# A two-block model on one core: the convolution's running sum, the norm's reciprocal and the one-hots' row of numbers move to PSUM, and the gates' copy writes runs of four

## The chip, the cores and the metric

The kernel runs on one core of a Trainium2 chip. TensorE (PE) multiplies matrices and writes to the PSUM memory; VectorE (DVE), ScalarE (ACT) and GpSimd (POOL) do elementwise work on SBUF and PSUM (POOL, here, on SBUF only); SyncE (SP) and ACT issue most DMAs. The metric is the device time of one execution in microseconds.

## The reference, cut to what matters

The model has 512 tokens of width 1024 and two blocks. The first block's mixer has a causal convolution of 31 taps over 384 channels, followed by a layer norm; then come a mixture of 32 experts, and the second block with two recurrent mixers (on more tokens of context) and a product-key expert layer. The two parts that the change touches:

```python
def hybrid_mixer(x, w_in, conv_a_w, conv_a_b, ln_a_g, ln_a_b, ...):
    z = x @ w_in
    a_val, a_gate, b_gate, c_gate, b_val, pool_in = jnp.split(z, IN_SPLITS, axis=-1)
    u = a_val * jax.nn.sigmoid(a_gate)
    u = causal_depthwise_conv(u, conv_a_w) + conv_a_b          # 31 taps, 384 channels
    y_a = jax.nn.silu(layer_norm(u, ln_a_g, ln_a_b))
    ...
    return jnp.concatenate([y_a, y_b, y_c], axis=-1) @ w_out

def _peer(h, w_query, sub_keys, expert_u, expert_v):           # 8 heads, 128 x 128 experts, 16 chosen per head
    q = (t @ w_query).reshape(n_tok, P_HEADS, 2, P_DQ)
    sc = jnp.einsum('thcd,hckd->thck', q, sub_keys)
    s1, i1 = lax.top_k(sc[:, :, 0], P_TOPK)
    s2, i2 = lax.top_k(sc[:, :, 1], P_TOPK)
    cand = (s1[..., :, None] + s2[..., None, :]).reshape(n_tok, P_HEADS, P_TOPK * P_TOPK)
    top_s, top_i = lax.top_k(cand, P_TOPK)
    ...
    gates = jax.nn.softmax(top_s)
    act = gelu(einsum('td,tkd->tk', tb, expert_u[eb])) * gb    # eb: the chosen experts, gb: their gates
    return jnp.einsum('tk,tkd->td', act, expert_v[eb])
```

## The kernel before

Everything is fp32; products that need it are made of two fp32r halves each (`split`: ACT casts the high half, DVE or POOL subtracts for the low half, line 117). The order of the instructions on each engine is set when the kernel is built: the scheduler of the tile framework takes the program and orders each engine's queue by its own estimates, and within it every instruction waits for the tiles it needs. A tile's buffer comes from a pool with a fixed number of buffers, and a new tile waits until the last reader of the old one is done.

**The mixer** (`mixer`). 17 units `z` of 128 channels come from TensorE (24 matmuls each, line 165). They rotate through the seven PSUM slots of the pool `mx_ps`, tag "z", as do the later tiles pp, stat and o. For each of three channel groups, za and zg give u = za*sigmoid(zg) (line 180, DVE), the first tap writes the running sum `ua` (line 181, TENSOR_SCALAR), and 30 more taps add to it in place (line 184, SCALAR_TENSOR_TENSOR: u shifted x the tap's column of weights + ua). u and ua both lie in the SBUF tile hT. Meanwhile POOL splits the weights of z (w1l), and works on the short convolution (b, ub). DVE also takes the pooled branch (lines 231 to 241), whose products are pp (line 247). Then `stat` sums ua over channels on TensorE (line 221), DVE subtracts the mean (254), a second `stat` gives the variance, line 258 its reciprocal root `rs`, and line 260 multiplies ua by rs, three times. The output product o (line 286) takes the chunks k = 4 to 7 first and those of ua last.

**The expert layer** (`Peer`). `queries` computes scores; `best` takes each key set's top 16, `select` a head's top 16 of 50 candidate pairs: it forms their sums (cand on DVE, cid, the pairs' numbers, on POOL), takes the best (top16), and looks their numbers up with a comparison `eq` against a row of numbers 0 to 49 (line 1891, DVE), times cid (line 1893, POOL), summed on DVE (pk_id, line 1898). `chosen` makes gates of them. Three of the four tiles of 128 tokens (0 to 2) go a dense way: `gates` builds for each four tokens two one-hot blocks, ohA (DVE line 1944, or ACT lines 1941 and 1942) and ohB (DVE line 1946), by comparing the row of numbers `iota` (SBUF, 0 to 127) with the tokens' expert numbers; POOL multiplies ohB by the gates (1947), TensorE multiplies both (gp, 1950), ACT copies gp to the SBUF tile gst (1951), which goes to DRAM as GD. `up` computes, ahead of need, the first GEB = 24 blocks of dots of the dense way (line 1966, needs uraw, uhi, ulo). After the gates, the dense loop over 128 expert blocks reads GD back (gch, a DMA of line 1988 on ACT's queue), multiplies it with ge (dact, dah) and sums y (line 2006) on TensorE, with dots of further blocks in between. Tile 3 goes another way: its experts are fetched by indirect DMAs (gu, gv) that POOL issues. In the program, tile 3's `best`, `select` and `chosen` stand between the gates and the dense loop; the pool `pr_d` of the dense loop (gch, dact) takes the SBUF that the selection's pool `pr_s` gives back.

Of the kernel before, what the change touches and what calls it, by code (L numbers as in the profile page):

```python
# [9 lines left out]
F = mybir.dt.float32  # L10
# [4 lines left out]
OP = mybir.AluOpType  # L15
AX = mybir.AxisListType
PSUM = bass.MemoryType.PSUM

P = 128
S = 512  # L20
# [32 lines left out]
def tcol(e, name, j=0, n=1):  # L53
    off, _ = TP[name]
    return e.tp[:, off + j:off + j + n]
# [64 lines left out]
def mixer(e):  # L120

    nc, tc, a = e.nc, e.tc, e.a
    ctx = ExitStack()
    pw = ctx.enter_context(tc.tile_pool(name="mx_w", bufs=1, reuse_waits="tile"))
    ps = ctx.enter_context(tc.tile_pool(name="mx_ps", bufs=7, space=PSUM))
# [43 lines left out]
    tmp = e.hT.rearrange("p k t -> p (k t)")  # L169
    u = tmp[:, 0:3 * (S + 30)].rearrange("p (i t) -> p i t", i=3)  # L170
    ua = tmp[:, 3 * (S + 30):3 * (2 * S + 30)].rearrange("p (i t) -> p i t", i=3)
    tmp2 = e.xpre.rearrange("p t d -> p (t d)")
    tmp = tmp2.rearrange("p (i t) -> p i t", i=8)
    sg2, sd, rs, sq = tmp[:, 0:3, :], tmp[:, 3, :], tmp[:, 4, :], tmp[:, 5:8, :]
    nc.vector.memset(u[:, :, 0:30], 0.0)
    for i in range(3):
        za, zg = z(), z()
        sg = pt.tile([P, S], F, name="sg")
        nc.scalar.activation(sg, zg, AF.Sigmoid)
        nc.vector.tensor_mul(u[:, i, 30:], za, sg)  # L180
        nc.vector.tensor_scalar(ua[:, i, :], u[:, i, 0:S], tcol(e, "conv_a_w", i * 31), tcol(e, "conv_a_b", i),
                                op0=OP.mult, op1=OP.add)
        for k in range(1, 31):
            nc.vector.scalar_tensor_tensor(ua[:, i, :], u[:, i, k:k + S], tcol(e, "conv_a_w", i * 31 + k),
                                           ua[:, i, :], op0=OP.mult, op1=OP.add)
    for v0 in v0s:
        nc.gpsimd.memset(v0[:, 0:16], 0.0)
        nc.scalar.copy(v0[:, 16:], z())
# [36 lines left out]
    for j in range(2):  # L225
# [3 lines left out]
        for lev in range(1, 3 + 2 * j):  # L229
# [4 lines left out]
            if g // 2 == j:  # L234
# [5 lines left out]
                                               op1=OP.subtract)  # L240
# [14 lines left out]
        nc.scalar.activation(sq[:, i, :], ua[:, i, :], AF.Square)  # L255
    va = stat(sq)
    nc.scalar.activation(sd, va, AF.Sqrt, bias=e.eps5)
    nc.vector.reciprocal(rs, sd)
    for i in range(3):
        nc.vector.tensor_mul(ua[:, i, :], ua[:, i, :], rs)  # L260
# [1480 lines left out]
NK = 16  # L1741
NC = 50
# [31 lines left out]
class Peer:  # L1774
# [11 lines left out]
    def open(self, ctx):  # L1786
        tc = self.e.tc
        mk = lambda nm, b, **kw: ctx.enter_context(tc.tile_pool(name=nm, bufs=b, reuse_waits="tile", **kw))
        self.pd = mk("pr_k", 1)
        self.s = self.pd.tile([P, NT, NH, 2, NK], F, name="pk_s")  # L1790
        self.ixu = self.pd.tile([P, NT, NH, 2, NK], U32, name="pk_iu")
        self.sc3 = self.pd.tile([P, 16, P], F, name="sc3", tag="sc3")
        self.pa = mk("pr_a", 2)
        self.sel_ctx = ExitStack()
        self.sel = self.sel_ctx.enter_context(tc.tile_pool(name="pr_s", bufs=2, reuse_waits="tile"))
        self.ts = self.sel.tile([P, NT, NH, NK], F, name="pk_ts", bufs=1)
        self.idf = self.sel.tile([P, NT, NH, NK], F, name="pk_id", bufs=1)
        self.psd = mk("pr_ps", 2, space=PSUM)

    def normed(self, t, x, pool, ps):  # L1800

# [70 lines left out]
    def select(self, tiles, h):  # L1872

        e, nc, pool, s = self.e, self.e.nc, self.sel, self.s
        n = tiles.stop - tiles.start
        ixf = pool.tile([P, NT - 1, 2, NK], F, name="pk_if")[:, 0:n]
        nc.vector.tensor_copy(ixf, self.ixu[:, tiles, h])
        cand = pool.tile([P, NT - 1, NC], F, name="cand")[:, 0:n]
        pair_sums(nc.vector, cand, s[:, tiles, h, 0, :], s[:, tiles, h, 1, :])
        i1 = pool.tile([P, NT - 1, NK], F, name="i1")[:, 0:n]  # L1880
        nc.vector.tensor_scalar(i1, ixf[:, :, 0, :], float(P), None, op0=OP.mult)
        cid = pool.tile([P, NT - 1, NC], F, name="cid")[:, 0:n]
        pair_sums(nc.gpsimd, cid, i1, ixf[:, :, 1, :])
        tu, tf = pool.tile([P, NT - 1, NK], U32, name="tu")[:, 0:n], pool.tile([P, NT - 1, NK], F, name="tf")[:, 0:n]
        for t in range(n):
            top16(e, pool, cand[:, t, :], self.ts[:, tiles.start + t, h, :], tu[:, t, :], "b")
        nc.vector.tensor_copy(tf, tu)
        eqs = []
        for t in range(n):
            eq = pool.tile([P, NK, NC], F, name="eq", bufs=6)  # L1890
            nc.vector.tensor_tensor(eq, self.iota[:, None, 0:NC].to_broadcast([P, NK, NC]),  # L1891
                                    tf[:, t, :, None].to_broadcast([P, NK, NC]), op=OP.is_equal)
            nc.gpsimd.tensor_mul(eq, eq, cid[:, t:t + 1, :].to_broadcast([P, NK, NC]))  # L1893
            eqs.append(eq)

        def rest():
            for t, eq in enumerate(eqs):
                nc.vector.reduce_sum(self.idf[:, tiles.start + t, h, :], eq, axis=AX.X)  # L1898

        return rest  # L1900
# [15 lines left out]
    def gates(self, t, idx, gt, pool, ps, ahead):  # L1916
# [14 lines left out]
        for hf in range(P // HT):  # L1931
            stg = pool.tile([P, P, HT], F, name="gst")
            for i in range(0, HT, 4):
                j = hf * HT + i
                if j % 32 == 0:
                    next(ahead, None)
                A = pool.tile([P, 4, P], F, name="ohA", bufs=3)
                io4 = self.iota[:, None, :].to_broadcast([P, 4, P])
                if (j // 4) % 4 < (1 if t == NT - 2 else 2):
                    for q in range(4):  # L1940
                        nc.scalar.activation(A[:, q], self.iota, AF.Square, bias=et[:, 3, j + q:j + q + 1])
                    nc.scalar.activation(A, A, AF.Relu, scale=-1.0, bias=1.0)
                else:
                    nc.vector.tensor_tensor(A, io4, et[:, 0, j:j + 4, None].to_broadcast([P, 4, P]), op=OP.is_equal)  # L1944
                B = pool.tile([P, 4, P], F, name="ohB", bufs=3)
                nc.vector.tensor_tensor(B, io4, et[:, 1, j:j + 4, None].to_broadcast([P, 4, P]), op=OP.is_equal)  # L1946
                nc.gpsimd.tensor_mul(B, B, et[:, 2, j:j + 4, None].to_broadcast([P, 4, P]))  # L1947
                gp = ps.tile([P, 4, P], F, name="gp", bufs=4)
                for q in range(4):
                    nc.tensor.matmul(gp[:, q, :], A[:, q], B[:, q], start=True, stop=True)  # L1950
                nc.scalar.copy(stg[:, :, i:i + 4].rearrange("p b t -> p t b"), gp)
            c = t * (P // HT) + hf
            nc.sync.dma_start(e.GD[0][c], stg[:, 0:GB0])
            for b in range(0, P - GB0, 40):
                nc.sync.dma_start(e.GD[1][c, :, b:b + 40], stg[:, GB0 + b:GB0 + b + 40])
# [122 lines left out]
def peer(e, pr, ctx):  # L2078
# [30 lines left out]
        rest.pop(0)()  # L2109
    rest.pop()()  # L2110
    idx, gt = pr.chosen(NT - 1, pr.pc)
    pr.sel_ctx.close()
    pool = ctx.enter_context(tc.tile_pool(name="pr_d", bufs=2, reuse_waits="tile"))
    psy = ctx.enter_context(tc.tile_pool(name="pr_y", bufs=1, space=PSUM))
# [138 lines left out]
```

## Time and profile before

| | before |
|---|---|
| median of 3 runs | 4354.65 us (4354.23 to 4362.32) |
| profiled execution, time | 4351.65 us |
| its span | 4349.5 us (2.15 us of its time lie outside) |
| mean granted TensorE clock | 0.973 |
| busy share PE / DVE / ACT / POOL | 94% / 75% / 48% / 26% |

The span is the time from the first to the last instruction of the profiled execution. An engine's busy share is a mean over stages that differ: which engine a stage waits for is to be read in that stage. The mixer fills about the first 180 us, the mixture of experts runs from about 285 us, the selection for tiles 0 to 2 ends near 3118 us, the gates run from there to 3356 us, and the dense loop to the end.

### The profile page before, as it was taken

Reading aid. Unit: us, or ns where it says so; the run is one execution under the profiler, and the core shown is the slowest. Engines: PE = TensorE matmul, PEld = TensorE weight load, DVE = VectorE, ACT = ScalarE, POOL = GpSimd, SP = SyncE. Lnnn points to the kernel's source line nnn. Section 1 sums busy time; section 2 is a strip of 40 time slices with the busy share of each in tenths; the row PEclk is TensorE's granted clock in tenths of the full one; section 3 lists DMA queues with packets and bytes.
Section 4 is the critical chain, followed back from the end, with each engine's and each line's share of the span. In section 5 each row is a group of like instructions: output and inputs, shape, how many; then the busy total and the mean of one; then the engine's idle time right before and its main releaser. Section 6 shows DMA issues by size and latency. Waiting matters only on the chain. (4 is left out here: it accounts for less than half of the span.)

```text
span 4349.5 us, 60160 instructions
## 1 busy us (share of the span) xinstructions
PE 4093.4 (94%) x22534; PEld 3256.5 (75%) x22534; DVE 3251.3 (75%) x5532; ACT 2072.3 (48%) x2876; POOL 1109.6 (26%) x929
## 2 busy tenths in 40 slices
PE   8799999999999979999999999989777999999998
PEld 7456666666666637888788788777676899999997
DVE  8868888888888875766667665547998577777777
ACT  3246666666666654434444344333477333333333
POOL 5311220220100030111001110016676344443431
PEclk9889999999999989999999999999889999999999
DMA  3379999999999863212322122432234888888884
GB/s 123 130 267 341 332 344 336 336 343 334 336 339 337 326 240 98 71 65 85 93 88 71 62 69 88 160 131 83 83 136 162 281 302 303 302 307 313 303 297 171
DMA packets 355415, 933.84 MB, mean 215 GB/s; under 512 B 60928, under 2 KB 169376, under 8 KB 322224
## 3 DMA queue, kind: packets, MB, share of 16 engines
q1 hardware_dynamic: 299168, 741.19, 48.4%
q0 software_dynamic: 49536, 176.18, 11.0%
q10 hardware_dynamic: 6416, 12.58, 0.9%
q8 instruction: 179, 2.93, 0.3%
q14 instruction: 116, 0.95, 0.1%
HBM read 865.66 MB, written 64.20 MB: 214 GB/s over the span
## 5 line engine op out<-in xcount | busy, mean ns | idle before, releaser
L117 DVE TENSOR_TENSOR wlo<-wraw,whi 128x2048 fp32r<-128x2048 f32 x384 | 872.3, 2290 | 101.5 <-ACT whi L116 100.8
L116 ACT CAST whi<-wraw 128x2048 fp32r<-128x2048 f32 x384 | 722.0, 1909 | 122.6 <-DMA wraw<-in_w_gate_up_dram 82.7
L1966 PE MATMUL dots<-hp_h,ulo 128*128 128x384 f32 x1024 | 355.9, 348 | 24.5 <-POOL ulo L117 22.6
L1966 PE MATMUL dots<-hp_h,uhi 128*128 128x384 f32 x1024 | 355.9, 348 | 2.2 <-ACT uhi L116 2.2
L1966 PE MATMUL dots<-hp_l,uhi 128*128 128x384 f32 x1024 | 354.6, 346 | 0.0
L2016 POOL DMA_INDIRECT gu<-in_expert_u_dram,idx x128 | 192.6, 1505 | 443.2 <-DVE gu L2026 412.0
L600 PE MATMUL gu<-wlo,xhi 128*96 128x512 f32 x1024 | 297.7, 410 | 0.0
L116 ACT CAST uhi<-uraw 128x1024 fp32r<-128x1024 f32 x128 | 134.2, 1049 | 315.9 <-PE dots L1966 239.6
L600 PE MATMUL gu<-whi,xhi 128*96 128x512 f32 x1024 | 283.8, 397 | 0.6 <-ACT xhi L116 0.6
L600 PE MATMUL gu<-whi,xlo 128*96 128x512 f32 x1024 | 279.9, 394 | 0.0
L2006 PE MATMUL y<-vhi,dah 128*128 128x512 f32 x762 | 238.4, 394 | 12.7 <-ACT dah L1997 12.7
L2006 PE MATMUL y<-vhi,dal 128*128 128x512 f32 x762 | 236.2, 391 | 0.0
L2006 PE MATMUL y<-vlo,dah 128*128 128x512 f32 x762 | 235.5, 390 | 0.0
L600 PEld LDWEIGHTS gu<-whi,xhi 128*96 128x96 f32 x1024 | 163.3, 162 | 73.8 <-ACT yx L634 4.4
L600 PEld LDWEIGHTS gu<-whi,xlo 128*96 128x96 f32 x1024 | 165.4, 162 | 70.5
L1966 PEld LDWEIGHTS dots<-hp_h,ulo 128*128 128x128 f32 x1024 | 197.8, 193 | 27.1 <-POOL ulo L117 24.2
L1998 DVE TENSOR_TENSOR dal<-dact,dah 128x384 fp32r<-128x384 f32 x127 | 70.9, 558 | 196.4 <-ACT dah L1997 196.3
L1997 ACT CAST dah<-dact 128x384 fp32r<-128x384 f32 x127 | 65.2, 513 | 319.3 <-issue 261.3
L600 PEld LDWEIGHTS gu<-wlo,xhi 128*96 128x96 f32 x1024 | 158.8, 162 | 66.5 <-issue 8.3
L1966 PEld LDWEIGHTS dots<-hp_h,uhi 128*128 128x128 f32 x1024 | 198.1, 193 | 6.8 <-ACT uhi L116 2.6
L1966 PEld LDWEIGHTS dots<-hp_l,uhi 128*128 128x128 f32 x1024 | 197.8, 193 | 4.2
L576 POOL DMA_INDIRECT xg<-H,slot_tok x32 | 38.8, 1212 | 632.9 <-PE mtp L569 428.6
(718 smaller groups left out, 10618.0 us busy)
## 6 DMA issues: line engine op xcount, KB each, us to landing
wraw<-in_w_gate_up_dram SPq DMA_DIRECT2D x256, 1024.0 KB, 5.9
wraw<-in_w_down_dram SPq DMA_DIRECT2D x128, 1024.0 KB, 7.2
uraw<-in_uT_dram SPq DMA_DIRECT2D x128, 512.0 KB, 5.3
vraw<-in_expert_v_dram SPq DMA_DIRECT2D x128, 512.0 KB, 3.9
wuraw<-in_w2p_dram SPq DMA_DIRECT2D x72, 512.0 KB, 3.3
GD<-gst SPq DMA_DIRECT2D x36, 640.0 KB, 4.6
gch<-GD SPq DMA_DIRECT2D x30, 768.0 KB, 12.2
piece<-in_w_ada_dram SPq DMA_DIRECT2D x24, 512.0 KB, 4.0
```

The source lines that it names most:

```text
L116: e.copied = e.nc.scalar.copy(hi, src).ins
L117: (eng or e.nc.vector).tensor_sub(lo, src, hi.bitcast(F))
L576: e.gathered = nc.gpsimd.indirect_dma_start(out=xg, out_offset=None, in_=e.H, in_offset=bass.IndirectOffsetOnAxis(ap=self.tok, axis=0)).ins
L600: nc.tensor.matmul(self.gu[n], l[:, k, :], r[:, cs], start=False, stop=k == KD - 1 and r is lo)
L1966: nc.tensor.matmul(dots, l[:, k, :], r[:, k, 0:ND], start=k == 0 and i == 0, stop=k == KD - 1 and i == 2)
L1997: nc.scalar.copy(ah, act)
L1998: self.anchor = nc.vector.tensor_sub(al, act, ah.bitcast(F)).ins
L2006: self.e.nc.tensor.matmul(y[t][:, cs], l[:, t * P:(t + 1) * P], r[:, cs], start=b == 0 and l is ah and r is hi, stop=b == P - 1 and l is al)
L2016: nc.gpsimd.indirect_dma_start(out=g, out_offset=None, in_=src, in_offset=bass.IndirectOffsetOnAxis(ap=idx[:, h, k:k + 1], axis=0))
```

## The change

Four edits. The running sum of the convolution is a PSUM tile `cacc` (tag "z", so it takes one of the seven slots while a channel group is summed); only the last tap writes SBUF. The reciprocal `rs` goes to a PSUM tile of the same tag. The row of numbers is copied once to a PSUM tile `io_ps`, and eq, ohA and ohB on DVE read that (ACT's form of ohA still reads iota in SBUF); it holds a PSUM buffer of its own until `chosen` for tile 3 is through. The gates' copy takes its elements in another order: for each of 128 columns four tokens, so that it writes runs of four floats to gst (16 B, 128 B apart) and reads PSUM with a stride of 128 elements; before, it read PSUM in order and wrote single floats 128 B apart. Lines shift by one to six.

```diff
--- before.py
+++ after.py
@@ -171,18 +171,19 @@
     ua = tmp[:, 3 * (S + 30):3 * (2 * S + 30)].rearrange("p (i t) -> p i t", i=3)
     tmp2 = e.xpre.rearrange("p t d -> p (t d)")
     tmp = tmp2.rearrange("p (i t) -> p i t", i=8)
-    sg2, sd, rs, sq = tmp[:, 0:3, :], tmp[:, 3, :], tmp[:, 4, :], tmp[:, 5:8, :]
+    sg2, sd, sq = tmp[:, 0:3, :], tmp[:, 3, :], tmp[:, 5:8, :]
     nc.vector.memset(u[:, :, 0:30], 0.0)
     for i in range(3):
         za, zg = z(), z()
         sg = pt.tile([P, S], F, name="sg")
         nc.scalar.activation(sg, zg, AF.Sigmoid)
         nc.vector.tensor_mul(u[:, i, 30:], za, sg)
-        nc.vector.tensor_scalar(ua[:, i, :], u[:, i, 0:S], tcol(e, "conv_a_w", i * 31), tcol(e, "conv_a_b", i),
+        acc = ps.tile([P, S], F, name="cacc", tag="z")
+        nc.vector.tensor_scalar(acc, u[:, i, 0:S], tcol(e, "conv_a_w", i * 31), tcol(e, "conv_a_b", i),
                                 op0=OP.mult, op1=OP.add)
         for k in range(1, 31):
-            nc.vector.scalar_tensor_tensor(ua[:, i, :], u[:, i, k:k + S], tcol(e, "conv_a_w", i * 31 + k),
-                                           ua[:, i, :], op0=OP.mult, op1=OP.add)
+            nc.vector.scalar_tensor_tensor(acc if k < 30 else ua[:, i, :], u[:, i, k:k + S],
+                                           tcol(e, "conv_a_w", i * 31 + k), acc, op0=OP.mult, op1=OP.add)
     for v0 in v0s:
         nc.gpsimd.memset(v0[:, 0:16], 0.0)
         nc.scalar.copy(v0[:, 16:], z())
@@ -255,6 +256,7 @@
         nc.scalar.activation(sq[:, i, :], ua[:, i, :], AF.Square)
     va = stat(sq)
     nc.scalar.activation(sd, va, AF.Sqrt, bias=e.eps5)
+    rs = ps.tile([P, S], F, name="rs", tag="z")
     nc.vector.reciprocal(rs, sd)
     for i in range(3):
         nc.vector.tensor_mul(ua[:, i, :], ua[:, i, :], rs)
@@ -1796,6 +1798,10 @@
         self.ts = self.sel.tile([P, NT, NH, NK], F, name="pk_ts", bufs=1)
         self.idf = self.sel.tile([P, NT, NH, NK], F, name="pk_id", bufs=1)
         self.psd = mk("pr_ps", 2, space=PSUM)
+        self.io_ctx = ExitStack()
+        psi = self.io_ctx.enter_context(tc.tile_pool(name="pr_io", bufs=1, space=PSUM, reuse_waits="tile"))
+        self.io_ps = psi.tile([P, P], F, name="io_ps")
+        self.e.nc.vector.tensor_copy(self.io_ps, self.iota)
 
     def normed(self, t, x, pool, ps):
 
@@ -1888,7 +1894,7 @@
         eqs = []
         for t in range(n):
             eq = pool.tile([P, NK, NC], F, name="eq", bufs=6)
-            nc.vector.tensor_tensor(eq, self.iota[:, None, 0:NC].to_broadcast([P, NK, NC]),
+            nc.vector.tensor_tensor(eq, self.io_ps[:, None, 0:NC].to_broadcast([P, NK, NC]),
                                     tf[:, t, :, None].to_broadcast([P, NK, NC]), op=OP.is_equal)
             nc.gpsimd.tensor_mul(eq, eq, cid[:, t:t + 1, :].to_broadcast([P, NK, NC]))
             eqs.append(eq)
@@ -1935,7 +1941,7 @@
                 if j % 32 == 0:
                     next(ahead, None)
                 A = pool.tile([P, 4, P], F, name="ohA", bufs=3)
-                io4 = self.iota[:, None, :].to_broadcast([P, 4, P])
+                io4 = self.io_ps[:, None, :].to_broadcast([P, 4, P])
                 if (j // 4) % 4 < (1 if t == NT - 2 else 2):
                     for q in range(4):
                         nc.scalar.activation(A[:, q], self.iota, AF.Square, bias=et[:, 3, j + q:j + q + 1])
@@ -1948,7 +1954,7 @@
                 gp = ps.tile([P, 4, P], F, name="gp", bufs=4)
                 for q in range(4):
                     nc.tensor.matmul(gp[:, q, :], A[:, q], B[:, q], start=True, stop=True)
-                nc.scalar.copy(stg[:, :, i:i + 4].rearrange("p b t -> p t b"), gp)
+                nc.scalar.copy(stg[:, :, i:i + 4], gp.rearrange("p t b -> p b t"))
             c = t * (P // HT) + hf
             nc.sync.dma_start(e.GD[0][c], stg[:, 0:GB0])
             for b in range(0, P - GB0, 40):
@@ -2109,6 +2115,7 @@
         rest.pop(0)()
     rest.pop()()
     idx, gt = pr.chosen(NT - 1, pr.pc)
+    pr.io_ctx.close()
     pr.sel_ctx.close()
     pool = ctx.enter_context(tc.tile_pool(name="pr_d", bufs=2, reuse_waits="tile"))
     psy = ctx.enter_context(tc.tile_pool(name="pr_y", bufs=1, space=PSUM))
```

The scheduler puts some instructions elsewhere. First, DVE at the start of the convolution (hT holds u and the finished sum, tp the weights; L180 is u of the next channel group). Before:

```order
L180 TENSOR_TENSOR hT<-z,sg 128x512
L181 TENSOR_SCALAR hT<-hT,tp 128x512
L184 SCALAR_TENSOR_TENSOR hT<-hT,tp 128x512 x12
L180 TENSOR_TENSOR hT<-z,sg 128x512
L184 SCALAR_TENSOR_TENSOR hT<-hT,tp 128x512
L181 TENSOR_SCALAR hT<-hT,tp 128x512
L184 SCALAR_TENSOR_TENSOR hT<-hT,tp 128x512 x34
L180 TENSOR_TENSOR hT<-z,sg 128x512
L184 SCALAR_TENSOR_TENSOR hT<-hT,tp 128x512
```

After:

```order
L180 TENSOR_TENSOR hT<-z,sg 128x512
L182 TENSOR_SCALAR cacc<-hT,tp 128x512
L185 SCALAR_TENSOR_TENSOR cacc<-hT,tp,cacc 128x512 x14
L180 TENSOR_TENSOR hT<-z,sg 128x512
L185 SCALAR_TENSOR_TENSOR cacc<-hT,tp,cacc 128x512
L182 TENSOR_SCALAR cacc<-hT,tp 128x512
L185 SCALAR_TENSOR_TENSOR cacc<-hT,tp,cacc 128x512 x28
L185 SCALAR_TENSOR_TENSOR hT<-hT,tp,cacc 128x512
L185 SCALAR_TENSOR_TENSOR cacc<-hT,tp,cacc 128x512
L180 TENSOR_TENSOR hT<-z,sg 128x512
L185 SCALAR_TENSOR_TENSOR cacc<-hT,tp,cacc 128x512
```

The taps of a channel group now write cacc, and the rows hT<-hT,tp,cacc are the last taps of the first two groups. u of the second group stands two taps later and that of the third two earlier, and the second group's first tap still stands among the taps of the first.

Second, DVE around the end of the gates: the last ohA and ohB, and what follows (eq, pk_id, tf, pk_if and tu belong to the selection for tile 3). Before:

```order
L1944 TENSOR_TENSOR ohA<-io,et 128x512
L1946 TENSOR_TENSOR ohB<-io,et 128x512
L117 TENSOR_TENSOR ulo<-uraw,uhi 128x1024
L117 TENSOR_TENSOR vlo<-vraw,vhi 128x1024 x3
L1991 TENSOR_TENSOR dact<-ge,gch 128x384 x2
```

After:

```order
L1950 TENSOR_TENSOR ohA<-io_ps,et 128x512
L1952 TENSOR_TENSOR ohB<-io_ps,et 128x512
L1897 TENSOR_TENSOR eq<-io_ps,tf 128x800 x2
L1904 TENSOR_REDUCE pk_id<-eq 128x16
L1893 CAST tf<-tu 128x16
L1904 TENSOR_REDUCE pk_id<-eq 128x16
L1897 TENSOR_TENSOR eq<-io_ps,tf 128x800
L1893 CAST tf<-tu 128x16
L1883 CAST pk_if<-pk_iu 128x32
L1770 MAX_INDEX tu<-pk_ts,cand 128x8
L1897 TENSOR_TENSOR eq<-io_ps,tf 128x800
L1904 TENSOR_REDUCE pk_id<-eq 128x16
```

Before, nothing of the selection was left behind the last ohB. Now all eight eq and all eight pk_id of tile 3, 14 sums cand, and the small operations between them and in `chosen` stand behind it, and the dense loop's vlo and dact behind these.

Third, POOL at the same place (ohB is its product with the gates, eq its product with cid; gu is the fetch of tile 3's experts). Before:

```order
L1893 TENSOR_TENSOR eq<-eq,cid 128x800
L1947 TENSOR_TENSOR ohB<-ohB,et 128x512 x5
L1893 TENSOR_TENSOR eq<-eq,cid 128x800
L1947 TENSOR_TENSOR ohB<-ohB,et 128x512 x40
L2016 DMA gu<-in_expert_u_dram,idx 128x1024 x17
```

After:

```order
L1953 TENSOR_TENSOR ohB<-ohB,et 128x512 x69
L1899 TENSOR_TENSOR eq<-eq,cid 128x800
L1758 TENSOR_TENSOR cid<-pk_if,i_28616 128x16
L1758 TENSOR_TENSOR cid<-pk_if,i_28616 128x8
L1758 TENSOR_TENSOR cid<-pk_if,i_28616 128x5
L1758 TENSOR_TENSOR cid<-pk_if,i_28616 128x4
L1758 TENSOR_TENSOR cid<-pk_if,i_28616 128x3
L1759 TENSOR_TENSOR cid<-pk_if,i_28616 128x6
L1761 TENSOR_TENSOR cid<-i_28616,pk_if 128x8
L1899 TENSOR_TENSOR eq<-eq,cid 128x800
```

The eight eq of tile 3 stood among the ohB, and 40 ohB followed the last of them; now 69 ohB come in a row, and all eight eq with six heads' sums cid follow behind, ahead of the fetches gu. On ACT, the exponential of `chosen` for tile 3 and a table load moved behind the last gst too, ahead of the casts vhi and the issue of gch. SP's order and TensorE's order of z, gp and dots are the same but for a few places.

## Rows read from the trace of the kernel before

**Rows 1.** The page: busy microseconds, share of the span and instructions of each engine.
```profile
PE 4093.4 (94%) x22534; PEld 3256.5 (75%) x22534; DVE 3251.3 (75%) x5532; ACT 2072.3 (48%) x2876; POOL 1109.6 (26%) x929
```

**Rows 2.** Stretches (us): length, busy (instructions) of PE, PEld, DVE, ACT, POOL; clock, DMA share, GB/s.
```profile
80.00:100.00 20.00, 19.79 (x87) 16.06 (x86) 20.00 (x14) 7.20 (x11) 16.72 (x9) 1.00 0.27 85
...
120.00:140.00 20.00, 5.83 (x9) 1.42 (x9) 16.40 (x30) 3.68 (x6) 3.07 (x3) 0.50 0.07 26
...
300.00:1550.00 1250.00, 1241.20 (x5483) 842.30 (x5482) 1055.97 (x764) 818.42 (x640) 188.66 (x92) 1.00 0.92 336
...
2975.00:3118.00 143.00, 119.28 (x568) 102.19 (x567) 134.31 (x672) 40.37 (x68) 97.41 (x88) 0.92 0.17 61
...
3118.50:3355.50 237.00, 182.81 (x1163) 167.28 (x1162) 228.89 (x427) 186.01 (x335) 168.58 (x159) 0.94 0.38 138
...
3374.50:4349.00 974.50, 962.47 (x4768) 867.88 (x4768) 715.35 (x939) 337.54 (x483) 350.65 (x254) 0.99 0.80 286
```

**Rows 3.** Lines 184 and 181: busy us and mean ns, then durations min/median/max in ns.
```profile
L184 DVE SCALAR_TENSOR_TENSOR hT<-hT,tp 128x512 f32<-128x512 f32 x90 | 101.2, 1173 | 0.8
...
L184 DVE SCALAR_TENSOR_TENSOR hT<-hT,tp x90: 734/751/2894, 23.2 to 134.7; 128x512 f32<-128x512 f32 x90
...
L181 DVE TENSOR_SCALAR hT<-hT,tp x3: 535/547/2628, 22.7 to 83.2; 128x512 f32<-128x512 f32 x3
```

**Rows 4.** Lines 260 and 180, min/median/max; timeline (start us, us) at 81 us.
```profile
L260 DVE TENSOR_TENSOR hT<-hT,xpre x3: 680/2841/2892, 154.7 to 161.2; 128x512 f32<-128x512 f32 x3
...
L180 DVE TENSOR_TENSOR hT<-z,sg x3: 676/689/691, 21.9 to 81.5; 128x512 f32<-128x512 f32 x3
...
81.13 1.64 POOL L117 TENSOR_TENSOR yl<-b,yh 128x512 fp32r<-128x512 f32 x1 [0.73 <-PE z L165]
...
81.54 0.68 DVE L180 TENSOR_TENSOR hT<-z,sg 128x512 f32<-128x512 f32 x1
```

**Rows 5.** Timeline of the front: start us, duration us, instruction.
```profile
102.99 0.39 PE L165 MATMUL z<-xh,w1l 128*128 128x512 f32 x1
...
129.18 6.26 DVE L184 SCALAR_TENSOR_TENSOR hT<-hT,tp 128x512 f32<-128x512 f32 x8
...
138.91 4.39 PE L221 MATMUL stat<-hT,ones 128*128 128x512 f32 x6
```

**Rows 6.** DVE's groups of lines from 2970 to 3118.5 us: busy us, mean ns.
```profile
L1891 DVE TENSOR_TENSOR eq<-io,tf 128x800 f32<-128x800 f32 x24 | 28.4, 1237 | 0.0
```

**Rows 7.** Groups of lines in the gates, 3118.5 to 3375 us: busy us, mean ns.
```profile
L1946 DVE TENSOR_TENSOR ohB<-io,et 128x512 f32<-128x512 f32 x96 | 95.5, 1018 | 1.1 <-PE gp L1950 1.1
L1944 DVE TENSOR_TENSOR ohA<-io,et 128x512 f32<-128x512 f32 x56 | 56.8, 1014 | 3.4 <-PE gp L1950 2.0 <-PE etp L1927 0.9
...
L1898 DVE TENSOR_REDUCE pk_id<-eq 128x16 f32<-128x800 f32 x8 | 7.7, 968 | 2.3 <-POOL eq L1893 2.3
...
L1951 ACT COPY gst<-gp 128x512 f32<-128x512 f32 x96 | 102.0, 1079 | 50.6 <-PE gp L1950 50.2
...
L1893 POOL TENSOR_TENSOR eq<-eq,cid 128x800 f32<-128x800 f32 x8 | 16.9, 2110 | 3.9 <-DVE eq L1891 3.9
L1756 POOL TENSOR_TENSOR cid<-pk_if,i 128x16 f32<-128x16 f32 (+4 forms) x40 | 10.5, 296 | 1.5 <-DVE i L1881 0.9 <-DVE pk_if L1877 0.3
```

**Rows 8.** Lines 1946 and 1891 over the whole span: durations min/median/max, first and last start.
```profile
L1946 DVE TENSOR_TENSOR ohB<-io,et x96: 673/681/2265, 3119.9 to 3355.9; 128x512 f32<-128x512 f32 x96
...
L1891 DVE TENSOR_TENSOR eq<-io,tf x32: 966/979/2551, 2974.1 to 3269.4; 128x800 f32<-128x800 f32 x32
```

**Rows 9.** ScalarE's copies at lines 1439 (reads PSUM with a stride) and 1444 (without).
```profile
L1439 ACT COPY bvT<-zv x16: 361/478/593, 1704.5 to 2657.9; 128x512 f32<-128x512 f32 x8, 128x256 f32<-128x256 f32 x8
...
L1444 ACT COPY bv<-bvt x16: 372/478/585, 1708.5 to 2659.3; 128x256 f32<-128x256 f32 x8, 128x512 f32<-128x512 f32 x8
```

**Rows 10.** The chain that ended last, at the end of the gates: start us, us, what.
```profile
3361.93 11.28 DMA gch<-GD
...
3374.58 5.48 PE y L2006 x16
```

## The prediction, on record before the changed kernel ran

> **What bounds the kernel now.** I read the page's busy shares first: TensorE is busy for 94% of the span, VectorE (DVE) for 75%, ScalarE (ACT) for 48%, GpSimd (POOL) for 26% [rows 1]. An edit to DVE and ACT work can therefore pay only in the stretches where TensorE is not full, so I looked for those in the table by stage [rows 2]. In the mixture-of-experts stage (300 to 1550 us) TensorE works 1241.2 of 1250 us and in the last one (from 3374.5) 962.5 of 974.5: a microsecond won earlier moves these stretches forward whole and shortens nothing in them. Two stages touched by the change are different. In the front, DVE is busy 20.00 of 20 us and TensorE in 120 to 140 us only 5.83. In the gates, 3118.5 to 3355.5 us, DVE is busy 228.9 of 237 us, ACT 186.0, TensorE 182.8. DVE ends last in both, so its own time is what can be won there.
>
> Next I asked why DVE's instructions take what they take. The convolution's 90 taps take 751 ns in the median, 2894 at worst, and 1173 in the mean, 101.2 us together [rows 3]. The stage table dates the slow ones: in 80 to 100 us, with POOL busy 16.72 us, DVE finishes 14 instructions; in 120 to 140, with POOL busy 3.07, it finishes 30 [rows 2]. The product with the reciprocal goes the same way: three of one shape, 680, 2841 and 2892 ns [rows 4]. All these have two tensors in SBUF as operands. The gate value za*sg, of the same size but with za in PSUM, takes 676 to 691 ns, and the third of them began at 81.54 us, in the middle of a POOL split (81.13 to 82.77), and still took 0.68 [rows 4]. So an instruction of which only one tensor operand is in SBUF seems not to be held up by POOL. The change makes the taps, the three products and the one-hots such instructions.
>
> **The front.** From the first tap at 23.2 us to the end of the last at 135.4 [rows 3, 5] DVE has 112.2 us: 101.2 of taps and 11.0 of the rest. If all 90 take the median, they cost 67.6 us; where each waits for the one before, eight take 6.26 us, 0.78 each [rows 5], which makes 70.4. With 11.0 less about 2 (of three first taps one took 2628 ns against 547 [rows 3]) the sum ends at 23.2 + 67.6 to 70.4 + 9 = 100 to 103 us. But the last z matmul ends only at 103.4 [rows 5], and nothing on TensorE behind it can be earlier. The running sums now also hold three of the seven PSUM slots in which z, pp and stat rotate, each for some 25 to 30 us: by counting 5.5 us for each z (24 matmuls; 87 are done in 20 us [rows 2]) a slot is wanted 2 to 5 us before its sum is through, twice, so z may end up to 7 us late; I take 2 to 3. Behind the last tap come the pool's last steps, pp and then stat, 3.5 us (135.4 to 138.91 [rows 5]). I get stat at 108 to 110 instead of 138.9: 30 us less. No row shows DVE writing to PSUM. Bounds: as fast as now at its best (0.75, stat then waits for z: 33 us) and 0.90 a tap, 0.12 above the dependent pitch (stat at 117: 22 us). I take a value near the first, because the nearest row is za*sg, 689 with a PSUM operand.
> The rule that speaks against this: the Trainium skill, "Perfetto Trace Analysis", section Optimizing Scalar/DVE Operations, has DVE's fixed access time at about 60 ns on SBUF and 125 on PSUM. By it 90 taps would cost an estimated 6 us more and 152 one-hots 10 more. The rows show no such step: 689 ns with a PSUM operand, 680 for the same size without [rows 4].
> The three products with the reciprocal fall from 6.4 to about 2.1 us [rows 4]; TensorE has other chunks of the output product to do meanwhile, so I count 2 of the 4.3. Front: **-32 us** (bounds 20 and 37). It is passed on, since what follows (the output product, router, weights' loads on the one SyncE queue) starts from it.
>
> **The selection for tiles 0 to 2** (before 3118 us). 24 comparisons eq take 1237 ns in the mean [rows 6] against a median of 979 [rows 8]: 24 x 0.26 = 6 us of DVE, which is busy 134.3 of 143 us there [rows 2]. I take **-5** (0 to 6).
>
> **The gates.** ohA and ohB are 152 instructions and 152.3 us [rows 7]; at the median of ohB, 681 ns [rows 8], they take 104: 48 us of DVE go. The copy of a gate block has 96 instructions of 1079 ns [rows 7]. Reading PSUM across costs ACT nothing visible: 593 ns at most where its copy reads with a stride, 585 where it doesn't [rows 9]. So what costs is its writing of single elements 128 B apart; with runs of four I take 0.6 us, 96 x 0.48 = 46 us less of ACT; the other bound is nothing.
> What is late next: TensorE. Its 182.8 us of work in that stretch [rows 2] don't shrink, ACT falls to 140, DVE to 181, and from DVE the order takes away more: the eight eq, their reductions and half of tile 3's sums now stand behind the last ohB, at least 17 us. With four engines handing on blocks through three or four buffers I don't expect the bare 183; I take **198** for first to last ohB (183 to 222) against 236 (3119.9 to 3355.9 [rows 8]).
> What is moved is not free. In the kernel before, the selection of tile 3 ran between the gates, and 18.7 us behind the last ohB the first y began: DVE, POOL and TensorE finish, GD is written, then gch is loaded, 11.28 us [rows 10]. Now eight eq, eight reductions, and some 40 small DVE operations stand behind it on DVE: 8 x (0.98 + 0.97) + 40 x about 0.3 = 28 us; on POOL eight products of 2.1 and 42 sums of up to 0.3 [rows 7], nearly 30 us. Each head passes from DVE to POOL and back, so they only partly overlap: **36 us** (28 to 44). The loads of gch and the gathers stand behind these on ACT's queue and on POOL; gch must wait as its buffer lies where the selection's tiles were. Hence last ohB to first y: 36 + 11.3 + about 1.5 for dact and dah = 49, against 18.7. TensorE has few dots left to fill it with, since ge has a fixed number of buffers.
> Sum: 198 + 49 = 247 against 254.7 (3119.9 to 3374.6): **-8 us** (bounds -31 and +24). The 48 us that the one-hots give are nearly eaten by the selection's new place.
>
> **Sum.** -32 - 5 - 8 = -45. The profiled execution took 4351.65 us (its span 4349.5 and 2.15 around it); 4306.7. The median of the runs shown lies 3.0 higher: **4310 us**.
>
> **Rivals.**
> (a) The gates fall to TensorE's floor and the new tail overlaps well: 185 + 28 + 13 = 226, -29 in place of -8. Total -66, 4289. For it: TensorE's 54 idle us of now (237 less 182.8) stand behind a DVE that then has room. Against it: only three buffers for each one-hot. Chance 0.15.
> (b) The tail takes all back: ACT's copy keeps its 1.08 us and the gates stay at 215, tail 44: 272, +17. Total -20, 4335. Chance 0.13.
> (c) The change does not do what it says: the second tensor operand is not what matters, since each tap reads its weight column from SBUF too. Taps, eq and one-hots stay as slow as now. Then the front and the selection give 0, and the gates only lose the moved 17 us: 219 + 49 = 268 against 254.7, in all +13, 4368; if half the slowness goes, about 4337. For it: the first tap, with one tensor and two columns in SBUF, was slow once too [rows 3]. Against it: za*sg. The page "SBUF — State Buffer" of the Trainium skill, section Who interferes with whom, has it as za*sg shows it: with one SBUF input no contention. Chance 0.06, half of it slower.
> (d) The other side: the sum's way through PSUM. Each tap must read what the one before just wrote. At 1.12 us (101.2 / 90) the front gains nothing; from 1.29 on it costs the 15 us that the rest gives, and the kernel is slower. At 1.4 us the taps take 126 and stat comes 25 us later than now: +10, 4365. For it: no row shows DVE writing there. Against it: its reads there, at 689. Chance 0.05.
>
> **The numbers.** The forecast has 0.61: front -24 to -35, stage of the gates -20 to +8, so 4290 to 4328. To hold 8 in 10, the range takes in (a) and most of (b): 4282 to 4337. A measurement of this kernel can tell about 0.2% (8.7 us) from no change. Faster: the forecast, (a) and (b), 0.88 with a little of each lost to "same"; same 0.05; slower 0.07.
>
> **What would show it.** Taps of 0.73 to 0.80 us with no value above 1.0; the last tap at 98 to 106 us; stat near 109; ohA and ohB under 0.72 in the mean; the gate copy near 0.6; the first to the last ohB some 198 us with TensorE as its busiest engine; then 30 us and more in which TensorE is all but idle, DVE and POOL alternate, and y starts 49 us behind the last ohB. It is wrong if taps have a pitch above 0.9, if z waits long for a slot, or if the tail does not come.

## Result and the profile after

The changed kernel takes 4264.45 us in the median of four runs (4259.45 to 4267.54), the one before 4355.86 in its four: 0.9784 of it, 95% interval 0.9769 to 0.9800, some 91 us less. The profiled execution spans 4262.4 us in place of 4349.5, 87.1 less. This is faster than the forecast of 4310 and than the range's lower end of 4282.

Where the 87 us come from can be read from first starts. The durations of the lines that answer to [rows 3, 4, 8], min/median/max in ns, first and last start in us (L185 is the taps, L182 the first ones, L262 the products with the reciprocal, L1952 ohB, L1897 and L1899 the eq on DVE and on POOL, L1957 the gates' copy, L1953 POOL's product of ohB):

```profile
L185 DVE SCALAR_TENSOR_TENSOR cacc<-hT,tp,cacc x87: 734/749/758, 24.6 to 101.6; 128x512 f32<-128x512 f32 x87
...
L185 DVE SCALAR_TENSOR_TENSOR hT<-hT,tp,cacc x3: 734/744/748, 56.0 to 102.4; 128x512 f32<-128x512 f32 x3
...
L182 DVE TENSOR_SCALAR cacc<-hT,tp x3: 802/807/814, 23.8 to 58.6; 128x512 f32<-128x512 f32 x3
...
L262 DVE TENSOR_TENSOR hT<-hT,rs x3: 671/676/678, 126.3 to 131.4; 128x512 f32<-128x512 f32 x3
...
L1952 DVE TENSOR_TENSOR ohB<-io_ps,et x96: 666/680/692, 3076.4 to 3248.9; 128x512 f32<-128x512 f32 x96
...
L1897 DVE TENSOR_TENSOR eq<-io_ps,tf x32: 962/975/982, 2940.9 to 3277.7; 128x800 f32<-128x800 f32 x32
...
L1899 POOL TENSOR_TENSOR eq<-eq,cid x32: 1728/1757/1825, 2942.0 to 3278.8; 128x800 f32<-128x800 f32 x32
...
L1957 ACT COPY gst<-gp x96: 564/585/597, 3079.9 to 3252.8; 128x512 f32<-128x512 f32 x96
...
L1953 POOL TENSOR_TENSOR ohB<-ohB,et x96: 1032/1040/2094, 3077.1 to 3249.7; 128x512 f32<-128x512 f32 x96
```

The first eq starts at 2940.9 us instead of 2974.1: the front gave 33.2. The first ohB starts at 3076.4 instead of 3119.9: 43.5, so the selection of tiles 0 to 2 gave 10.3. None of the DVE instructions that have one operand in PSUM is ever slow now: the worst tap takes 758 ns (2894 before), the worst ohB 692 (2265), the worst eq 982 (2551). POOL's own instructions are faster too: its eq take 1757 ns in the median, where before they took 2174, and the eight in the gates 2110 in the mean [rows 7]. The gates' copy is at 585.

The timeline of the front, which answers to [rows 5] (start, duration):

```profile
103.60 0.39 PE L165 MATMUL z<-xh,w1l 128*128 128x512 f32 x1
...
105.62 1.22 DVE L242 TENSOR_TENSOR xpre<-pm,pv 64x16 f32<-64x16 f32 x1
...
109.82 2.89 PE L222 MATMUL stat<-hT,ones 128*128 128x512 f32 x3
```

The last z matmul ends at 104.0, 0.6 later than before; the slots that the sums hold cost next to nothing. The last tap ends at 103.1, stat starts at 109.8 in place of 138.9. From the last tap to stat it is now 6.7 us, where it was 3.5: DVE first waits 1.9 us for a pp that stands behind z on TensorE, and of the last steps of the pooled branch two (L242, with two tensors in SBUF) take 1.22 and 1.23 us beside POOL's instructions of the short convolution, where they took 0.16 and 0.17 before.

The table by stage, which answers to [rows 2]: the gates from first to last ohB, from there to the first y, and the dense loop:

```profile
3076.40:3249.60 173.20, 161.45 (x1142) 151.29 (x1141) 149.69 (x366) 144.02 (x329) 106.31 (x109) 1.00 0.50 186
...
3249.60:3287.00 37.40, 8.63 (x55) 8.30 (x53) 32.94 (x80) 8.33 (x11) 25.45 (x54) 0.64 0.40 135
...
3287.00:4262.00 975.00, 962.85 (x4768) 868.05 (x4768) 715.85 (x939) 338.89 (x483) 350.08 (x254) 0.99 0.80 287
```

The gates take 172.5 us from the first to the last start of ohB instead of 236, TensorE is busy 161.5 us there, and its granted clock is 1.00, the upper one of its two levels (1.2 and 2.4 GHz) throughout. Before it was 0.94 in the mean: slices of 20 us between 3180 and 3280 had 0.83 or 0.91, after one in which TensorE was busy for 12.96 us of 20, and from 3280 on it was 1.00 again. Behind the last ohB the first y starts 38 us later (18.7 before), and for 29 of these TensorE idles. The dense loop is the same 975 us. First ohB to first y: 210.6 us, 44.1 less than the 254.7 of before.

The groups of lines in the gates that show who waits (the first is TensorE's gp in the kernel before), and the chain behind the changed gates that ended last:

```profile
L1950 PE MATMUL gp<-ohB,ohA 128*128 128x128 f32 x760 | 105.9, 289 | 52.5 <-POOL ohB L1947 44.0 <-ACT ohA L1942 8.1
...
L1956 PE MATMUL gp<-ohB,ohA 128*128 128x128 f32 x754 | 98.7, 280 | 11.7 <-POOL ohB L1953 8.7 <-ACT ohA L1948 1.5 <-ACT ohA L1947 0.7
...
L1950 DVE TENSOR_TENSOR ohA<-io_ps,et 128x512 f32<-128x512 f32 x56 | 38.2, 682 | 17.1 <-PE gp L1956 16.9
```

```profile
3250.72 1.72 POOL eq L1899
...
3253.66 1.73 POOL eq L1899
...
3255.41 0.99 DVE pk_id L1904
...
3256.40 0.90 DVE eq L1897
...
3257.39 1.74 POOL eq L1899
...
3259.15 0.99 DVE pk_id L1904
...
3272.47 2.69 DVE ulo L117
...
3279.13 1.56 DVE pgt L1919
...
3280.72 4.92 DMA gch<-GD
...
3287.02 5.16 PE y L2012 x13
```

What the reader is to see: in the gates DVE now waits 16.9 us for gp, that is, for TensorE to release one-hot buffers, where it hardly waited before [rows 7], and TensorE waits only 8.7 us for POOL's ohB, where it waited 44.0. Behind the last ohB the chain alternates between POOL's eq and DVE's pk_id, eq and small sums until 3280.7, as the order said, and then loads gch in 4.92 us, not in the 11.28 of [rows 10].

### The profile page after: what moved, and what is told of

The parts are those of the page before. It is cut to its first block, busy times and chain, and to the rows that moved or that the text cites. A ratio compares the mean times of both kernels' runs of the same rounds, so it can differ in the third digit from the quotient of the medians.

```text
span 4262.4 us, 60165 instructions
## 1 busy us (share of the span) xinstructions
PE 4069.3 (95%) x22534; PEld 3240.0 (76%) x22534; DVE 3162.1 (74%) x5533; ACT 2033.2 (48%) x2876; POOL 1047.8 (25%) x929
```

## The experiments

All are built from the kernel before or the changed one, by the edit shown. Ratios are to the kernel before, of runs on the same chip.

**The front alone.** The first two edits, without io_ps and the copy.

> Only the running sum and the reciprocal go to PSUM. If the second SBUF operand is what POOL holds up: all taps 0.73 to 0.76 us, first stat 29 us earlier, the total 33 us below the kernel before, and the selection and the gates as before. Rival, in which the front's gain is partly taken back later by the loads: less than 25 us.

4318.51 us, 0.9914 (0.9897 to 0.9930); its span is 4317.0, 32.5 below. Durations of the taps and of eq:

```profile
L185 DVE SCALAR_TENSOR_TENSOR cacc<-hT,tp,cacc x87: 732/749/757, 24.2 to 101.2; 128x512 f32<-128x512 f32 x87
...
L1893 DVE TENSOR_TENSOR eq<-io,tf x32: 966/978/2547, 2938.6 to 3236.1; 128x800 f32<-128x800 f32 x32
```

The taps are as in the full change, eq as before, with its first start 35.5 us earlier. The front is worth its 33 us by itself, and nothing takes it back.

**The row of numbers alone.** The third edit, with the gates' copy as before.

> Only the row of numbers goes to PSUM; the gates' copy still takes 1.08 us. The scheduler's order has the selection of tile 3 behind the gates, as in the full change. If ACT then bounds the gates (its 144 us plus 96 x 0.49 = 191): first to last ohB about 195 us, the total 10 + 41 - 19 = 32 us below before. Rival, in which ACT has room enough: 173 us as in the full change, the total 54 below. In both the selection of tiles 0 to 2 gains 10 us, and POOL's ohB falls from 1.36 to about 1.04 in the median.

4317.42 us, 0.9911 (0.9894 to 0.9927). Its gates in the table by stage, then TensorE's gp and ACT's copy there:

```profile
3112.90:3303.80 190.90, 163.77 (x1148) 150.94 (x1147) 149.27 (x366) 179.06 (x329) 106.39 (x109) 1.00 0.45 170
...
L1954 PE MATMUL gp<-ohB,ohA 128*128 128x128 f32 x759 | 98.2, 280 | 27.1 <-ACT ohA L1946 22.3 <-POOL ohB L1951 4.1
...
L1955 ACT COPY gst<-gp 128x512 f32<-128x512 f32 x94 | 100.4, 1092 | 10.1 <-PE gp L1954 9.6
```

First to last ohB is 190.2 us. DVE and POOL are as in the full change; ACT is busy 179 of 191 us, and TensorE waits 22.3 us for one-hots that ACT builds. So ACT bounds these gates, as the first theory had it; the total is 38 us below (it had 32).

**The copy alone.** The fourth edit.

> Only the gates' copy changes. It falls to 0.59 us. If DVE alone bounds the gates of before, the total moves by 0 to -5 us. Rival, in which ACT's slow copy holds back the gp buffers and the one-hots on ACT: -15 us or more.

4354.41 us, 0.9992 (0.9982 to 1.0001): nothing that can be told. The copy does fall:

```profile
L1951 ACT COPY gst<-gp x96: 566/586/602, 3129.0 to 3363.8; 128x512 f32<-128x512 f32 x96
...
L1946 DVE TENSOR_TENSOR ohB<-io,et x96: 673/682/2246, 3125.4 to 3360.6; 128x512 f32<-128x512 f32 x96
```

45 us of ACT work go, and ohB still spans 235 us. With the slow one-hots DVE sets the pace, and ACT's time is worth nothing.

**Both edits of the expert layer.** The third and the fourth.

> The row of numbers and the gates' copy, without the front's two edits. If the parts add: 54 us below before (10 in the selection, 44 in the gates), first to last ohB 173 us and y 38 us behind. If the front's shift changed the gates: another number than 54.

4296.74 us, 0.9865 (0.9849 to 0.9881). Alone the two gave 0.9911 x 0.9992 = 0.9903; together they give 0.0038 of 4355 us, 17 us, more. The gates span 172.5 us here too, 17.7 less than with the slow copy. Times the front's 0.9914 it gives 0.9780, the full change within its interval: front and expert layer add.

**The running sum in a tile of its own, but in SBUF.**

```diff
+        acc = pt.tile([P, S], F, name="cacc")
-        nc.vector.tensor_scalar(ua[:, i, :], u[:, i, 0:S], ...
+        nc.vector.tensor_scalar(acc, u[:, i, 0:S], ...
-            nc.vector.scalar_tensor_tensor(ua[:, i, :], u[:, i, k:k + S], ..., ua[:, i, :], ...)
+            nc.vector.scalar_tensor_tensor(acc if k < 30 else ua[:, i, :], u[:, i, k:k + S], ..., acc, ...)
```

> The running sum has a tile of its own as in the change, but in SBUF; all else as before. If what counts is that a tap has two tensors in SBUF: taps near 1.17 us in the mean with values of 2.9, the total within 5 us of before. Rival, in which the tile of its own (no update in place) or the order counts: taps at 0.75, stat 29 us earlier, the total 30 us below.

4355.08 us, 0.9995 (0.9985 to 1.0004). The taps:

```profile
L185 DVE SCALAR_TENSOR_TENSOR cacc<-hT,tp,cacc 128x512 f32<-128x512 f32 x87 | 98.2, 1174 | 0.7
...
L185 DVE SCALAR_TENSOR_TENSOR cacc<-hT,tp,cacc x87: 734/750/2891, 22.8 to 133.5; 128x512 f32<-128x512 f32 x87
```

The mean is 1174 ns, as before, with the worst at 2891. Neither the new tile nor the last tap's own output counts; the place of the operand does.

**POOL writes only.** In the kernel before, the low halves of the mixer's weights are left out from the third unit on: POOL fills them with zeros.

```diff
-        split(e, r, hi, lo, nc.gpsimd if u > 1 else nc.vector)
+        if u > 1:
+            e.copied = nc.scalar.copy(hi, r).ins
+            nc.gpsimd.memset(lo.bitcast(F), 0.0)
+        else:
+            split(e, r, hi, lo, nc.vector)
```

> The kernel before, in which POOL fills the low halves of the mixer's weights from the third unit on with zeros instead of subtracting (it leaves that part of the product out): POOL still works for each unit, but these instructions read nothing from SBUF. If POOL's reads are what holds up the taps: no tap beside such a fill above 1.0 us, the mean falls from 1.17 to about 0.9 (what is left is beside the short convolution's POOL instructions). Rival, in which any POOL instruction holds them up: 1.1 or more.

One run: 4334.48 us, with the first stat at 111.7 us instead of 138.9. The mean tap, and the timeline of POOL and DVE from 37 to 77 us (taps are L188, the fill L147, the product ub L199):

```profile
L188 DVE SCALAR_TENSOR_TENSOR hT<-hT,tp 128x512 f32<-128x512 f32 x90 | 68.5, 814 | 0.8
...
37.28 15.99 DVE L188 SCALAR_TENSOR_TENSOR hT<-hT,tp 128x512 f32<-128x512 f32 x24
...
37.80 0.95 POOL L147 MEMSET w1l<- 128x1024 f32 x1 [4.49 <-PE z L169]
...
43.24 0.96 POOL L147 MEMSET w1l<- 128x1024 f32 x1 [4.49 <-PE z L169]
...
48.68 0.95 POOL L147 MEMSET w1l<- 128x1024 f32 x1 [4.48 <-PE z L169]
...
63.52 11.35 DVE L188 SCALAR_TENSOR_TENSOR hT<-hT,tp 128x512 f32<-128x512 f32 x17
...
66.30 10.34 POOL L199 TENSOR_TENSOR ub<-b,b 128x512 f32<-128x512 f32 x1 [0.35 <-ACT b L198]
...
75.40 1.79 DVE L188 SCALAR_TENSOR_TENSOR hT<-hT,tp 128x512 f32<-128x512 f32 x1
```

24 taps take 15.99 us, 0.67 each, across three fills: these POOL instructions, which read nothing, hold up no tap. The rival falls. What is left of the slow taps (814 ns in the mean) stands beside the short convolution's POOL instructions, which read.
The last three rows I had not expected. POOL's product ub, which reads two tensors, began at 66.30 and took 10.34 us, while the run of 17 taps that had begun before it went on at 0.67 each, none delayed; only the tap at 75.40 took 1.79. In the changed kernel the same product takes 1.30. So I read the collision as two-sided: either the tap or the POOL instruction waits, and here POOL waited for a whole run of taps.

**The selection of tile 3 ahead of the gates of tile 2.** The full change, and the block from `best` to `chosen` moved up in the program; nothing of it is left behind the last ohB.

```diff
             if t == NT - 2:
                 raws = [pr.raw_rows(b) for b in range(3)]
+                for c in range(16):
+                    pr.best(pr.sel, pr.sc3[:, c], NT - 1, c)
+                rest = [pr.select(slice(NT - 1, NT), 0)]
...
+                idx, gt = pr.chosen(NT - 1, pr.pc)
             pr.gates(t, *pr.chosen(t, pr.sel), pool, ps, ahead)
```

> The full change, with the selection of tile 3 put into the program ahead of the gates of tile 2, so that nothing of it is left behind the last ohB. DVE then has 150 + 33 = 183 us of work in the gates: first to last ohB about 187, y 19 behind, so 206 in place of 211: 5 us below the full change. Rival one, in which the selection only fills DVE's idle 23 us and TensorE bounds: 175 + 19, 17 below. Rival two, in which its chain over DVE and POOL holds the one-hots up: 200 or more, the total above the full change.

4274.79 us, 0.9809 (0.9796 to 0.9822), not below the full change. Its gates, TensorE's two longest waits in them together, the place of the longer one (16.07 us; the two ohB on both sides of it and a stretch within it), and the chain behind the gates:

```profile
3072.50:3276.70 204.20, 173.90 (x1184) 161.34 (x1183) 176.10 (x439) 149.87 (x334) 128.32 (x159) 0.95 0.44 163
...
L1972 PE MATMUL dots<-hp_h,ulo 128*128 128x384 f32 x141 | 49.9, 355 | 18.1 <-DVE ulo L117 18.1
...
3196.97 0.68 DVE L1952 TENSOR_TENSOR ohB<-io_ps,et 128x512 f32<-128x512 f32 x1
...
3207.00:3222.00 15.00, 0.31 (x2) 0.00 (x0) 14.73 (x51) 0.94 (x1) 11.46 (x33) 0.58 0.04 16
...
3223.38 0.69 PE L1972 MATMUL dots<-hp_h,ulo 128*128 128x384 f32 x1 [16.07 <-DVE ulo L117]
...
3230.60 0.68 DVE L1952 TENSOR_TENSOR ohB<-io_ps,et 128x512 f32<-128x512 f32 x1
...
3276.07 0.61 DVE ohB L1952
...
3282.33 12.67 DMA gch<-GD
...
3296.37 3.78 PE y L2012 x8
```

The gates last 203.5 us in place of 172.5, and the first y comes 20 us behind the last ohB in place of 38. Rival two has the numbers, and the rows show how: from 3196.97 to 3230.60 us, 33.6 us, no ohB starts. In between DVE works through the eq, pk_id and small sums of tile 3, nearly in one piece; TensorE has dots until 3207 and then stands still, 0.31 us busy of 15. In the full change no two ohB start more than 4.3 us apart. So the selection did not fill DVE's idle time between one-hots: in the order as it was built it stands as a block ahead of tile 2's gates, and they wait for its end. Also, gch takes 12.67 us again when it is issued right behind the writes of GD; behind the selection it took 4.92.

**The same ahead of the gates of tile 1.**

> As the run before it, with the selection of tile 3 ahead of the gates of tile 1. With twice the gates to spread over, the same sum of DVE work: between 0 and 10 us below the one with tile 2. Rival: no difference, since DVE's 183 us bound both.

4282.70 us, 0.9827 (0.9814 to 0.9841), gates of 206.8 us. More gates to spread over did not help, against my expectation, because the selection was not spread: here too it stands in one piece, no ohB starts from 3133.17 to 3167.32 us (34.2), and in that time TensorE waits 28.2 us in one go for the numbers of the next tile's experts (ef), which DVE casts behind it.

**The low halves ulo on POOL**, without and with the moved selection, and every second of them (`0 < b < 8 or b % 2`, also with the moved selection):

```diff
-            ge[b] = pr.up(b, nc.gpsimd if 0 < b < 8 else None)
+            ge[b] = pr.up(b, nc.gpsimd if 0 < b < GEB else None)
```

> The full change, with the low halves ulo of all blocks ahead of the dense loop subtracted by POOL instead of by DVE after the eighth. In the gates this takes 21 us from DVE (150 of 173 busy) and gives POOL about 38 (106 of 173), and two of them leave the selection behind the gates. If TensorE bounds the gates: they stay near 173 and the tail loses 4 us: -4 against the full change. Rival, in which POOL's ohB then come late: +10 or more.

4275.60 us, 0.9829 (0.9816 to 0.9843): the gates grew from the full change's 172.5 to 182.9 us, as the rival had it, with TensorE waiting 11.1 us for POOL's ohB instead of 8.7, and 4.2 us for ACT's ohA. The tail did not lose its 4 us either: the first y comes 38.4 us behind the last ohB, in the full change 38.1.

> The selection of tile 3 ahead of the gates of tile 2, and all ulo on POOL. In the run with the selection alone TensorE waited 18 us for ulo behind the selection on DVE. If DVE's queue is what made those gates 204 us long: they fall to about 183, y 20 behind, 8 us below the full change. Rival, in which the chain of the selection over DVE and POOL holds the one-hots up: they stay above 195 and nothing is won.

4286.68 us, 0.9845 (0.9831 to 0.9858), gates of 210 us. TensorE in them:

```profile
L1956 PE MATMUL gp<-ohB,ohA 128*128 128x128 f32 x755 | 100.9, 284 | 19.9 <-POOL ohB L1953 14.2 <-ACT ohA L1948 4.7
...
L1972 PE MATMUL dots<-hp_h,ulo 128*128 128x384 f32 x143 | 52.1, 365 | 9.2 <-POOL ulo L117 5.7 <-DVE ulo L117 3.4
```

The wait for DVE's ulo fell from 18.1 us to 3.4, and waits for POOL's ohB and ACT's ohA are longer. But the block of the selection stayed: no ohB starts for 36.3 us (3206.14 to 3242.43). So this run does not clear DVE's queue; it moves ulo out of it and leaves in it what holds the one-hots up.

> As the run before it, but only every second ulo on POOL after the eighth. If DVE is the bound, half the effect: gates of some 193 us; if POOL is the bound in the run before it, this one is the faster of the two.

4275.18 us, 0.9825 (0.9812 to 0.9839), gates of 210 us as well, and 34.8 us without an ohB. So the first theory's 193 us do not come. Of the second no more can be told than that the median is 11.5 us below the run before while the intervals of the two ratios overlap.

**Half of the selection ahead of the gates of tile 2**, all of `best` and four of the eight heads.

> The full change, with the top 16 of tile 3 and the selection of four of its eight heads ahead of the gates of tile 2, the other four behind the gates. Three eq and three pk_id leave the place behind the last ohB. If selection work costs the gates what it saves behind them: first to last ohB 185 to 190, y 25 to 28 behind, the total within 5 us of the full change. Rival, in which part of it fits into DVE's 23 idle us: gates 175 to 178 and the total 6 to 10 us below the full change.

4260.43 us, 0.9793 (0.9780 to 0.9807): the same as the full change. The gates span 179.1 us and y starts 30 behind: 209.4 us from the first ohB to the first y, against 210.6. Neither theory has these numbers (185 to 190 with 25 to 28, or 175 to 178): the gates lose 6.6 us and the tail gains 7.8. The longest time without an ohB is 11.9 us. No version was found that clearly beats the full change.

## Why the prediction was wrong, point by point

**The mechanism was right.** A second tensor operand in SBUF is what makes a DVE instruction and a POOL instruction that reads collide: the taps stay slow with their sum in SBUF, and fast in PSUM or when POOL only writes. The step on the front, -32, measured 33; stat was forecast for 108 to 110 and came at 109.8. That stat fits so well is luck: z was to end 2 to 3 us late and ended 0.6 late, and the 3.5 us that were to follow became 5.8. Rivals (c) and (d) are out: no tap is above 0.758 us, reading and writing PSUM.

**The selection, -5, gave 10.3.** I counted only DVE's eq. Their 24 fell from 28.4 us [rows 6] to 22.1 in the full change and in the two kernels that have the row of numbers in PSUM without the front's edits: the 6 that I had. POOL's eq went from 2236 to 1756 ns in the mean in this stretch, and DVE's pk_id waits 4.3 us for them instead of 6.7, another 2.4. The last 1.6 us I can't place. The collision was costed on one of its two engines.

**The gates, -8, gave 44.** This is the step that failed, in two terms.
First, I had TensorE's 182.8 us of work in that stretch not shrink, and took 198 for the gates. It shrank to 161.5, and the gates took 172.5. I had read TensorE's busy time as work. It was taken at a granted clock of 0.94, with blocks of gp that came singly and waits between them; now the clock is 1.00 in the stretch, a dots matmul takes 349 ns in the mean instead of some 375, and some 16 dots matmuls are done later. By an estimate the clock is worth 11 of the 21 us (6% of 182.8); no run splits the rest, and none shows why the clock stayed up. The kernel with the slow copy has TensorE's busy time down to 163.8 us already, at a clock of 1.00, though TensorE still waits 27 us in it. The other engines add 11 us to TensorE's 161.5, not 15 to 183. That ACT's copy matters was right, and the two kernels with the row of numbers in PSUM show for how much: 190 us with the slow copy, 172.5 with the fast one. Alone it gave nothing.
Second, the tail, 49 us, was 38. The selection took 32 of the forecast 36, and the load of gch 4.92 where I took the 11.28 from [rows 10]: in the kernel before, and again with the selection moved up (12.67), gch was issued right behind GD's last writes; behind the selection these have long landed. The other hardware queue moved 3.68 MB from 3361 to 3374 us of the kernel before, and 0.08 MB from 3280 to 3287 of the changed one, so the load was nearly alone; that this made it short is read from these rows, no run tests it. By this the tail gives back part of what it delays. The two terms, 25.5 and 11 us, are the 36 by which this stage was missed; with 5 for the selection and 1 for the front they make up the 42 us by which the profiled execution (4264.27 us) lies below 4306.7.

"The 48 us that the one-hots give are nearly eaten by the selection's new place" is false: the stage gave 44.1. As a block among the gates the same selection costs them 31 us (172.5 to 203.5), as much as it takes behind them, and saves only 18 there (38 to 20). With half of it at each place nothing changes either. Rival (a), with 226 us for this stage, was the nearest; even the sum's lower bound, -31 (183 + 28 + 12.8 = 223.8), was 13 us too high. One sum in the prediction does not come out: with its own terms (front -24 to -35, selection -5, gates -20 to +8) the forecast's stretch is 4295 to 4334 and not 4290 to 4328; the measured time lies below both.

**What stays open.** Whether the kernel gets faster with an order in which the selection of tile 3 is spread between the one-hots, into the 23 us that DVE idles in the gates of the full change: in all four kernels with the whole selection moved up it stands nearly in one piece, 33.6 to 36.3 us without an ohB. No run shows either why the gates grow by 10 us when POOL takes the low halves ulo: TensorE waits 5 us more in them and is busy 5 us more (166.5).

## What to carry to other kernels

Where a VectorE instruction with two tensors in SBUF runs beside GpSimd work that reads SBUF, look at the spread of its durations; if it is wide, one operand in PSUM takes the collision from both engines, and both gains belong in the sum. TensorE's busy time read at a lower clock and with gaps is no floor: here it fell from 182.8 us to 161.5. Work moved to where an engine has idle time in sum does not fill it when it stands in the engine's queue as one block. And two edits that each relieve one engine of a chain must be costed together: here one of them alone gave nothing, and 17 us on top of the other.

## What was not expected of the hardware

A POOL product of 128 x 512 took 1.30 us beside taps that read PSUM and 1.74 beside taps that read SBUF (line 195 of the kernel before, 1.733 to 1.739); and 10.34 when a run of such taps without a break stood beside it. DVE's accumulation in PSUM, writing and reading it in each step, is as fast as in SBUF (749 against 751 ns); the first tap, a TENSOR_SCALAR with one tensor operand, is slower with its output in PSUM, 807 against 547 ns, when nothing collides. ACT's copy with a stride of 128 elements on the PSUM side takes 585 ns, and 1079 with single floats 128 B apart on the SBUF side.
